# Neighbourhood attention: keys grouped by column strips, tokens reordered, nine second-stage units by seven products, an uneven share of filler

## The chip, the cores and the metric

One core of a Trainium2 chip runs the whole program. It has five engines that run their own instruction queues in order and meet by semaphores: TensorE (matmuls, written PE in the profile, its weight loads PEld), VectorE (DVE), ScalarE (ACT), GpSimd (POOL) and SyncE (SP), which here issues nearly all DMAs. Matmul results land in PSUM, in eight banks; everything else that the engines read or write lies in SBUF. The metric is the device time of one execution in microseconds; the time before is the median of three runs.

## The reference

One layer: an RMS norm, a projection of 1024 columns to q, k, v and a gate, a 2-D neighbourhood attention over a grid of 32 rows by 64 columns (2048 tokens, 16 heads of 64), a SiLU gate, an output projection with the residual, and a last RMS norm. A query sees 8 rows by 16 columns of keys, with a bias by relative position.

```python
h = rmsnorm(x, g)
proj = h @ w_in
q, k, v, gate = jnp.split(proj, 4, axis=-1)
# per query row r, keys of 8 rows from clip(r - 4), per 16 query columns 32 key columns
s = jnp.einsum('bnqhd,bknjhd->bhnqkj', qr, kr) * scale
s = jnp.where(col_valid, s + bias, NEG_INF)
p = jax.nn.softmax(s over all its keys)
o = jnp.einsum('bhnqkj,bknjhd->bnqhd', p, vr)
x = x + (o * jax.nn.silu(gate)) @ w_out
return rmsnorm(x, norm_f)
```

## The kernel before

All large products are done in three matmuls each (high by high, high by low, low by high part of float32 values rounded to float32r).

**Projection units.** A unit is 256 output columns of one kind: k, q and g (the gate) have four each, numbered j = 0 to 3, for two head pairs each; v has its own code. The 2048 tokens form four chunks c of 512. Stage one (`stage_one`) makes v and all twelve units for chunks 0 and 1, stage two (`stage_two`) makes v and the units of `units_two` for chunks 2 and 3. Both go through `seven_products`: a Strassen-Winograd scheme that gets a unit's 2 x 2 blocks (two column halves by two chunks) from seven block products of 4 x 3 matmuls of 128x512, with sums formed ahead on VectorE (`sum_`, `form`) and behind (`keep`, `add`, `out_`, `evac`). `give` splits or gates a result and stores it to DRAM with a lag. In stage one the results are multiplied by the reciprocal norm `rb[c]` on the way.

**Direct units.** The (kind, j, chunk) in `halves` that stage two leaves out are projected directly by `projections` and `group`: 24 matmuls for each column half and chunk. They are not done at once: together with the output projection (`outputs`) they are the *filler* of the attention.

**Attention.** `order` lists (head pair p, row block T); T counts 8 grid rows, whose keys lie in 11, 15, 15 or 12 rows (`KEY_ROWS`). First T = 0 for all eight pairs, then T = 1 and 2, then T = 3. Each entry gives two steps, of two column blocks C of 16 query columns each; so there are 64 steps and two more in which the last work runs out. A block C of 128 queries sees 24 or 32 key columns (`KEY_COLS`). Step i of the main loop does, in program order:

- `begin(i)`: loads for later steps are put on the SP queue (`load_k`, `load_e`, `load_v`, `load_sg`, each with a lag counted in filler matmuls), and `bias` adds mask and position table on GpSimd, L970;
- `feed`: filler matmuls, `amount[i]` of them in three portions, with `middle(i)` (query split `split_q`, next query load) between; the last portion goes on into an overdraft of up to 12 matmuls until 8 have passed since the last evacuation was issued (`calm`);
- `normalise(i - 1)`: the reciprocals of the softmax sums on VectorE (L1004) and the scaling on GpSimd (L1006);
- `turns(i - 2)`: transposes of the probabilities into PSUM (L1011), copied to SBUF by VectorE (L1036) and ScalarE (L1035);
- `scores(i)`: twelve matmuls (L988), then bias and negated maximum by one VectorE operation each (L995) and exponentials with sums on ScalarE (L998);
- `values(i - 2)`: the products with v (L1056), and in each odd step the gate multiplication (L1070) and the store of the result.

Transposes and products with v work on blocks of 4 key rows by 24 or 32 key columns, so the probabilities' contraction has 96 or 128 lines, and 72 or 96 where a block has only three rows; those are copied separately. For such blocks v must lie with rows and columns of one block in the partitions: `copy_v` copies v in DRAM from `vd` to `vc` once for each head pair, column block and half (64 DMAs in stages one and two), and `load_v` loads one tile for each column block. The tokens come in natural order for the projections; q and the gate are rearranged to blocks of 16 columns while they are evacuated (`tiled`, `blocked`), by runs of 16 values.

**Output.** `outputs` makes 16 tiles of 128 tokens: a tile's gated result is loaded and split (`split_og`, L1128 and L1129), 48 matmuls follow (L1250 to L1254) in two halves, `add_rows` adds the residual (L1161), and `finish` stores three later pieces of work with lags of 12, 24 and 44 filler matmuls: the reciprocal root of the last norm (`root`, eight small VectorE operations), the scaling (`scale`) and the two stores (`send`).

The order of the filler against the attention is a hand-written credit count:

```python
early = 96 * (12 - len(units_two)) + 192
amount = [early / 48] * 48 + [(384 - 30) / 18] * 18
```

With three units in `units_two` that is 1056 / 48 = 22 matmuls in each of the first 48 steps and 19.7 in the last 18.

## Time and profile before

| | |
|---|---|
| median of three runs | 1084.95 us (1084.85 to 1085.42) |
| the profiled execution | 1086.36 us, of it span 1084.5 us |
| granted TensorE clock | 0.999 |
| busy: TensorE, VectorE, ScalarE, GpSimd | 1071.1, 703.2, 531.2, 357.9 us |
| v of stage one, its products | 0 to 96 us, 96 to 327 us |
| v of stage two, its products | 327 to 414 us, 414 to 471 us |
| attention with filler | 471 to 1027 us |
| last output tiles | 1027 to 1084 us |

A profile row names a line of the kernel, an engine, an operation and the tiles written and read, with the count, the busy time, the mean length of one, and the idle time of the engine just before them with what ended it. A row of the table by stage has, for a stretch of the span, the busy time of each engine and the number of instructions in it, then the granted clock, the busy share of the DMA engines and the GB/s they moved. In the timeline a row begins with the start and the length; what stands in brackets is the idle time of the engine before it and what it had waited for.

### The profile page before, as it was taken

The numbers are of one execution on the slowest core, as the hardware profiler recorded it, in microseconds if no ns is written. First come the engines' busy times: TensorE is split into PE (matmuls) and PEld (weight loads), VectorE is DVE, ScalarE is ACT, GpSimd is POOL, SyncE is SP. The second block draws the span as 40 slices with busy tenths as digits, with TensorE's granted clock in tenths as the row PEclk, the third lists the DMA queues.
The fourth block names the chain that finished last, engine by engine and source line by source line (L and its number), as shares of the span: only waits on it lengthen the run. The fifth ranks groups of instructions, "written<-read, shape, count | busy, mean of one in ns | idle before, by whom it ended". The sixth has DMA issues, their size and how long they took to land.

```text
span 1084.5 us, 21929 instructions
## 1 busy us (share of the span) xinstructions
PE 1071.1 (99%) x7657; PEld 877.1 (81%) x7657; DVE 703.2 (65%) x1644; ACT 531.2 (49%) x1345; POOL 357.9 (33%) x474
## 2 busy tenths in 40 slices
PE   9999999999999999999999999999999999999997
PEld 6888888888888888887888888888888787888885
DVE  5376778778997535576555555664676786776643
ACT  7545334333434334346555555564576565665431
POOL 0000222312221000017545534444447656566200
PEclk9999999999999999999999999999999999999999
DMA  9633557574764366889868876886899787887442
GB/s 313 212 97 106 202 173 210 163 232 146 256 188 143 108 172 170 258 277 310 245 205 267 253 216 204 255 269 200 246 319 294 230 268 231 274 262 226 126 149 78
DMA packets 145901, 231.90 MB, mean 214 GB/s; under 512 B 13824, under 2 KB 61184, under 8 KB 145792
## 3 DMA queue, kind: packets, MB, share of 16 engines
q1 hardware_dynamic: 145648, 230.25, 68.2%
q8 instruction: 61, 1.00, 0.4%
q14 instruction: 48, 0.39, 0.1%
q10 hardware_dynamic: 144, 0.26, 0.1%
HBM read 171.73 MB, written 73.40 MB: 226 GB/s over the span
## 4 chain that ended last, share of the span: by engine, by line
PE 92%; DVE 3%; DMA 1%; ACT 1%; issue 1%; SPq 0%; POOL 0%; ACTq 0%; DVEq 0%; POOLq 0%
PE pp L411 23%; PE pv L531 16%; PE o L1056 8%; PE s L988 6%; PE pp L359 6%; PE pp L357 6%; PE pp L355 6%; PE po L1254 6%; PE po L1252 5%; PE po L1250 5%; PE ph L1011 5%; PE zp L1269 1%; DMA k_hi<-hi 1%; DMA land<-in_xt_dram 0%; DVE f L394 0%
## 5 line engine op out<-in xcount | busy, mean ns | idle before, releaser
L1006 POOL TENSOR_SCALAR x<-x,st 128x360 f32<-128x360 f32 (+5 forms) x256 | 143.0, 578 | 235.0 <-DVE st L1004 192.3
L970 POOL TENSOR_TENSOR em<-e,mk 128x480 f32<-128x480 f32 (+5 forms) x160 | 136.3, 886 | 138.3 <-DMA raw<-in_xt_dram 135.0
L998 ACT ACTIVATE x<-x,st 128x360 f32<-128x360 f32 (+5 forms) x256 | 151.8, 595 | 44.4 <-DVE st L995 44.4
L411 PE MATMUL pp<-h,f 128*128 128x512 f32 x480 | 155.4, 389 | 0.0
L430 POOL TENSOR_TENSOR tmp<-tmp,rb 128x512 f32<-128x512 f32 x36 | 58.9, 1637 | 270.6 <-DVE tmp L428 223.7
L411 PE MATMUL pp<-t,f 128*128 128x512 f32 x540 | 130.0, 390 | 0.3 <-DVE u L422 0.2
L995 DVE CUSTOM_DVE_ANT_0 x<-s,em 128x360 f32<-128x360 f32 (+5 forms) x256 | 124.0, 539 | 5.3 <-PE s L988 1.4
L411 PEld LDWEIGHTS pp<-t,f 128*128 128x128 f32 x540 | 101.2, 188 | 22.2 <-DVE u L422 1.2
L359 PE MATMUL pp<-h,w 128*128 128x512 f32 x288 | 115.1, 400 | 0.0
L357 PE MATMUL pp<-l,w 128*128 128x512 f32 x288 | 113.2, 393 | 0.0
L355 PE MATMUL pp<-h,w 128*128 128x512 f32 x288 | 113.1, 393 | 0.0
L1035 ACT ACTIVATE pta<-ph 96x256 f32<-96x256 f32 (+1 forms) x224 | 58.5, 333 | 104.3 <-PE ph L1011 104.3
L1036 DVE COPY pta<-ph 128x384 f32<-128x384 f32 (+3 forms) x128 | 60.7, 514 | 72.7 <-PE ph L1011 72.5
L411 PEld LDWEIGHTS pp<-h,f 128*128 128x128 f32 x480 | 90.1, 188 | 18.8
L1254 PE MATMUL po<-wol,gh 128*128 128x512 f32 x252 | 100.3, 398 | 0.0
L1252 PE MATMUL po<-woh,gl 128*128 128x512 f32 x252 | 98.9, 393 | 0.0
L1250 PE MATMUL po<-woh,gh 128*128 128x512 f32 x252 | 98.9, 392 | 0.0
L1056 PEld LDWEIGHTS o<-pta,vt 96*64 96x64 f32 (+2 forms) x1792 | 83.6, 137 | 17.2 <-issue 10.2
L1056 PE MATMUL o<-pta,vt 96*64 96x128 f32 (+4 forms) x1792 | 92.3, 254 | 1.4 <-DVE pta L1036 1.0
L411 PE MATMUL pp<-l,f 128*128 128x512 f32 x240 | 93.4, 389 | 0.0
L531 PE MATMUL pv<-wh,h 128*128 128x512 f32 x256 | 88.1, 390 | 0.0
L531 PE MATMUL pv<-wh,l 128*128 128x512 f32 x256 | 88.0, 389 | 0.0
(148 smaller groups left out, 1916.6 us busy)
## 6 DMA issues: line engine op xcount, KB each, us to landing
raw<-in_wg_dram SPq DMA_DIRECT2D x126, 256.0 KB, 5.1
e<-in_rpb_dram SPq DMA_DIRECT2D x54, 240.0 KB, 3.9
vt<-vc SPq DMA_DIRECT2D x64, 192.0 KB, 3.7
row<-in_xr_dram SPq DMA_DIRECT2D x32, 256.0 KB, 4.3
vd<-v SPq DMA_DIRECT2D x32, 256.0 KB, 3.0
k_hi<-hi SPq DMA_DIRECT2D x32, 256.0 KB, 2.6
k_lo<-lo SPq DMA_DIRECT2D x32, 256.0 KB, 3.8
vc<-vd SPq DMA_DIRECT2D x32, 256.0 KB, 4.4
```

Source lines behind the costliest of these rows:

```text
L355: nc.tensor.matmul(p, wh[w, b][:, cols], hh[k, c], start=(k == 0), stop=False)
L357: nc.tensor.matmul(p, wh[w, b][:, cols], hl[k, c], start=False, stop=False)
L359: nc.tensor.matmul(p, wl[w, b][:, cols], hh[k, c], start=False, stop=(k == NK - 1))
L411: nc.tensor.matmul(B[n, P], t[:, int(m == 2), c], x[k][int(m == 1)], start=P in (1, 6, 5) and k == 0 and m == 0, stop=k == 3 and m == 2, s ...
L531: nc.tensor.matmul(ps[t], a[:, o], b, start=k == 0 and m == 0, stop=k == NK - 1 and m == 2)
L970: (nc.gpsimd if attending[0] or not s else nc.vector).tensor_tensor(sh(t), E[p, s][:, u0 + 4:u1 + 4, v0 + 8:v1 + 8], sh(MK[0][:, m0:m0 + n ...
L998: nc.scalar.activation(X[i, C][s], X[i, C][s], AF.Exp, bias=st[:, s:s + 1], scale=-1.0, accum_out=st[:, 2 + s:3 + s])
L1006: nc.gpsimd.tensor_scalar(X[i, C][s], X[i, C][s], st[:, 4 + s:5 + s], 0.5, op0=OP.mult, op1=OP.mult)
L1056: nc.tensor.matmul(o[s * 64:s * 64 + 64, C * 128 + q0:C * 128 + q0 + nq], vt[C][:k, g - g0_, s * 64:s * 64 + 64], t[:k, at:at + nq], start ...
L1250: nc.tensor.matmul(p, gh, woh[q, j], start=(i == 0), stop=False)
L1252: nc.tensor.matmul(p, gl, woh[q, j], start=False, stop=False)
L1254: nc.tensor.matmul(p, gh, wol[q, j], start=False, stop=(i == NK - 1))
```

## The change

Seven things are changed together.

1. **Strips.** Keys are grouped by strips of 8 key columns over all key rows of the row block (11, 15 or 12), so a contraction has 88, 120 or 96 lines. `blocks(T)` becomes `strips(C)`; a column block has three or four strips, of which two concern all 128 queries and the others one half. Scores read k, and `bias` its table, by strips; `turns` copies each half in one operation; the queries of a block are ordered by two halves of 8 columns.
2. **Token order.** The host hands x over with the 64 columns of a grid row in the order (column within a strip, strip). v stored in this order already has, for each key row and column within a strip, its eight strips side by side, so `load_v` takes one tile of 8 strips for a head pair and row block, straight from `vd`; `copy_v`, `vc` and their 64 DMAs are gone, and the pool `vp` has two tiles of 1024 in place of four of 512.
3. **Evacuations.** k, q and the gate are put into their final order when PSUM is read (`of`, `lay`), now with a stride of 8 values; `rb` of chunks 0 and 1 is kept in k's order first and in the order of q and gate after `reorder_rstd`. Stage one therefore makes the four k units first. The gate multiplication of the attention needs no rearranging.
4. **Nine units in stage two.** `units_two` has j = 0 to 2, and `halves` only j = 3.
5. **Uneven filler.** 8.5 matmuls in each of the first 28 steps (and 8 more in each of the first three), the rest of the 480 evenly over the next 20, the last 18 as before.
6. **Overdraft.** 4.25 in place of 12.
7. **Roots.** While the attention runs, `root` is not queued with a lag but waits in a list for the next odd step (or the last steps), where `run_roots` runs it after 45% of the step's filler; scaling and stores follow 9 and 27 matmuls later.

```diff
-def blocks(T):
...
+def strips(C):
     out = []
+    for s in range(KEY_COLS[C][0] // 8, KEY_COLS[C][1] // 8):
+        halves = [h for h in range(2) if abs(2 * C + h - s) <= 1]
+        out.append((s, s - KEY_COLS[C][0] // 8, halves[0] * 64, len(halves) * 64))
     return out
...
+def reorder_rstd(c):
+    t = rbp([128, 512], F32, "rb")
+    nc.scalar.activation(t.rearrange("p (s r c) -> p s r c", r=8, c=8),
+                         rb[c].rearrange("p (r s c) -> p s r c", s=8, c=8), AF.Copy)
+    rb[c] = t
...
-    units_two = [(k, j) for j in range(1) for k in "kqg"]
-    halves = [(k, j, 1, c) for j in range(1, 4) for g in (("k", "q", "g") if j < 3 else ("k", "qg")) for c in (2, 3) for k in g]
+    units_two = [(k, j) for j in range(3) for k in "kqg"]
+    halves = [(k, j, 1, c) for j in range(3, 4) for g in ("k", "qg") for c in (2, 3) for k in g]
...
+    def of(kind, t):
+        return t.rearrange("p (r c s) -> p r s c", c=8, s=8) if kind == "k" else t.rearrange("p (n s) -> p s n", s=8)
+
+    def lay(kind, t):
+        return t.rearrange("p (r s c) -> p r s c", s=8, c=8) if kind == "k" else t.rearrange("p (s n) -> p s n", s=8)
...
-            nc.vector.tensor_tensor(U[n, i], B[n, P], U[n, 1], OP.add)
+            nc.vector.tensor_tensor(lay(kind, U[n, i]), of(kind, B[n, P]), lay(kind, U[n, 1]), OP.add)
...
-        us = [(k, j) for j in range(4) for k in "kqg"]
+        us = [("k", j) for j in range(4)] + [(k, j) for j in range(4) for k in "qg"]
...
-            if m and i in (1, 3, 5):
-                copies(0, 1)
+            if (m, i) == (4, 0):
+                reorder_rstd(0)
+                reorder_rstd(1)
...
+    def load_v(p, T):
         r0, r1 = KEY_ROWS[T]
+        must(*[("v", p // 4, t) for t in range(r0 // 2, (r1 + 1) // 2)])
+        rows = vd[p // 4][p % 4].rearrange("(k s) d -> k s d", s=8)[8 * r0:8 * r1]
+        VT[p, T] = t = vp([128, 1024], F32, "vt").rearrange("p (s d) -> p s d", s=8)
+        nc.sync.dma_start(t[:8 * (r1 - r0)], rows)
...
-                    nc.tensor.matmul(pst[s], qq[a, qs], kk[a, :r1 - r0, c0:c1], start=(m == 0), stop=(m == 2))
+                    nc.tensor.matmul(pst[s], qq[a, qs], kk[a, :r1 - r0, c0:c1].rearrange("p r (s c) -> p s r c", c=8), start=(m == 0), stop=(m == 2))
...
             for h in range(2):
-                four = sum(b[2] == 4 for b in halves_[h])
-                k = 4 * width(C)
+                n = len(halves_[h])
                 put = (lambda o, i_: nc.scalar.activation(o, i_, AF.Copy)) if h else nc.vector.tensor_copy
-                put(slots[:k, h, :2 * four], ph[h][:k, :128 * four].rearrange("p (n q) -> p n q", q=64))
-                if four < len(halves_[h]):
-                    k = halves_[h][four][2] * width(C)
-                    put(slots[:k, h, 2 * four:2 * four + 2],
-                        ph[h][:k, 128 * four:128 * four + 128].rearrange("p (n q) -> p n q", q=64))
+                put(slots[:k, h, :2 * n], ph[h][:k, :128 * n].rearrange("p (n q) -> p n q", q=64))
...
-        store(("y", n), 12, root)
-        store(("y", n), 24, scale)
-        store(("y", n), 44, send)
+        if ended[0]:
+            store(("y", n), 12, root)
+            store(("y", n), 24, scale)
+            store(("y", n), 44, send)
+        else:
+            roots.append((clock[0] + 8, n, root, scale, send))
+
+    roots = []
+    ended = [False]
+
+    def run_roots():
+        while roots and (roots[0][0] <= clock[0] or ended[0]):
+            _, n, root, scale, send = roots.pop(0)
+            root()
+            store(("y", n), 9, scale)
+            store(("y", n), 27, send)
...
-    amount = [early / 48] * 48 + [(384 - 30) / 18] * 18
+    first = 8
+    amount = [8.5] * 28 + [(early - 3 * first - 8.5 * 28) / 20] * 20 + [(384 - 30) / 18] * 18
+    calm_debt = amount[0] / 2
+    for i in range(3):
+        amount[i] += first
...
-        while credit[0] > 0 or credit[0] > -12 and clock[0] - state["event"] < calm:
+        while credit[0] > 0 or credit[0] > -calm_debt and clock[0] - state["event"] < calm:
...
-        if 0 < i <= N:
-            p, T, cs = pairs[i - 1]
-            later_loads(load_v(p, T, cs[0]) + load_v(p, T, cs[1]), 0, 2)
+        if i % 2 == 0 and i < N:
+            load_v(*order[m])
...
         quiet[0] = i % 2 == 1 or i >= N
+        if quiet[0]:
+            run_roots()
```

More of the change, by code (lines that the diff above doesn't have):

```diff
@@ L93, in build, with vh @@
     qp = pool("qp", 4)
-    vp = pool("vp", 4)
+    vp = pool("vp", 2)
+    vhalf = []
+    def vh(shape, dt, nm):
+        if not vhalf:
+            t = vp([128, 1024], dt, nm)
+            vhalf.extend((t[:, :512], t[:, 512:]))
+        return vhalf.pop(0)
     sp = pool("sp", 2)
@@ L627, in also @@
                     split_v(0, 1, 1)
-                    L2["x12"] = [vp([128, 512], F32, "land") for _ in range(4)]
+                    L2["x12"] = [vh([128, 512], F32, "land") for _ in range(4)]
                     for k in range(4):
@@ L792, in pair @@
                     do[b]()
-                if u and ts != (12,) and b % 2:
-                    copies(1, 1)
         def both(*fs):
@@ L1006, in normalise, with split @@
                 nc.gpsimd.tensor_scalar(X[i, C][s], X[i, C][s], st[:, 4 + s:5 + s], 0.5, op0=OP.mult, op1=OP.mult)
-    def turn(dst, i, C, s, blk, q0, nq):
-        g, lr, nr = blk[:3]
-        w = width(C)
-        nc.tensor.transpose(dst[:nr * w], X[i, C][s][q0:q0 + nq, lr * w:(lr + nr) * w],
-                            ident[q0:q0 + nq, q0:q0 + nq])
-    def split(T):
-        bl = blocks(T)
-        return [b for b in bl if b[4] == 128], [b for b in bl if b[4] == 64]
+    def split(C):
+        return [b for b in strips(C) if b[3] == 128], [b for b in strips(C) if b[3] == 64]
     def turns(i):
         p, T, cs = pairs[i]
-        full, part = split(T)
-        halves_ = [full + [b for b in part if b[3] == 64 * h] for h in range(2)]
+        k = 8 * (KEY_ROWS[T][1] - KEY_ROWS[T][0])
         for C in cs:
+            full, part = split(C)
+            halves_ = [full + [b for b in part if b[2] == 64 * h] for h in range(2)]
             t = PT[i, C] = pa([128, 768], F32, "pta")
@@ L1047, in values @@
         o = O[p, T]
-        g0_ = KEY_ROWS[T][0] // 4
-        vt = {C: VT.pop((p, T, C)) for C in cs}
+        vt = VT[p, T]
         for C in cs:
@@ L1356, in build @@
             values(i - 2)
+    ended[0] = True
+    store(("roots",), 8, run_roots)
     while next(outs, 0) != 0:
@@ L1377 @@
         "x": np.ascontiguousarray(xp),
[L1378 to L1379 removed]
+        "xr": np.ascontiguousarray(xc),
+        "xt": np.ascontiguousarray(xc.T),
         "wg": np.ascontiguousarray(wg),
```

122 lines of the change are left out of this document (45 added, 77 removed).

## The prediction

> **What bounds the kernel now.** I read the busy time of each engine first, then the same by stage, then the chain of waits, then single steps of the attention in order of time.
>
> ```profile
> PE 1071.1 (99%) x7657; PEld 877.1 (81%) x7657; DVE 703.2 (65%) x1644; ACT 531.2 (49%) x1345; POOL 357.9 (33%) x474
> ```
> ```profile
> core 0: us, PE busy (x) PEld busy (x) DVE busy (x) ACT busy (x) POOL busy (x), PEclk, DMA share, GB/s
> ...
> 96.00:315.00 219.00, 218.65 (x964) 180.39 (x963) 181.49 (x269) 84.02 (x163) 54.04 (x33) 1.00 0.61 190
> ...
> 416.00:471.00 55.00, 55.00 (x245) 45.53 (x244) 32.16 (x49) 16.66 (x29) 3.44 (x4) 1.00 0.81 249
> ...
> 490.00:623.00 133.00, 131.77 (x1244) 108.00 (x1243) 71.85 (x242) 75.79 (x239) 73.98 (x119) 1.00 0.82 257
> 623.00:803.00 180.00, 179.91 (x1869) 147.65 (x1869) 105.67 (x300) 101.90 (x297) 81.87 (x114) 1.00 0.77 241
> ```
> TensorE sets the end in every stage: 218.65 of 219 us in stage one's products, 55 of 55 in stage two's, 179.91 of 180 in the middle of the attention. Every other engine has room there, most of all in the attention, where VectorE is busy 105.67 of 180 us. So a matmul less is a matmul's time less, as long as the others keep up with a TensorE that comes round sooner.
>
> The price of one 128x512 matmul, from a stretch of the chain in stage two, and from two filler matmuls of the attention with seven issue intervals between them:
> ```profile
> 414.20 54.41 PE pp L411 x240
> ```
> ```profile
> 647.33 0.39 PE L355 MATMUL pp<-h,w 128*128 128x512 f32 x1
> ...
> 648.92 0.39 PE L357 MATMUL pp<-l,w 128*128 128x512 f32 x1
> ```
> 54.41 / 240 = 0.227 us, and 1.59 / 7 = 0.227 us: the same in both stages (the 0.39 us are one matmul's length, the matmuls overlap).
>
> **The change, part by part.**
>
> *Six more units by seven products.* A unit done directly takes 4 groups of 24 matmuls, 96; by seven products 7 x 12 = 84. Units go from three to nine, so 6 x 12 = 72 matmuls vanish: 72 x 0.227 = **16.3 us less**. It is certain by count. It is also a move: the attention loses 576 matmuls of filler (130.7 us) and stage two gains 504 (114.3 us). Stage two's units now take 55 us for three with VectorE at 32.16, so six more fit there under TensorE; I cost that at nothing.
>
> *The attention's steps get short.* A step (two query blocks of one head pair and row block) is filler, transposes, scores, products with v. Its own work on TensorE is read between the last filler matmul before it and the first after it, in a step with 11 key rows and in one with 15:
> ```profile
> 540.17 0.39 PE L357 MATMUL pp<-l,w 128*128 128x512 f32 x1
> ...
> 543.50 0.50 PE L359 MATMUL pp<-h,w 128*128 128x512 f32 x1
> ```
> ```profile
> 640.99 0.39 PE L357 MATMUL pp<-l,w 128*128 128x512 f32 x1
> ...
> 644.93 0.50 PE L359 MATMUL pp<-h,w 128*128 128x512 f32 x1
> ```
> ```profile
> L1056 PE MATMUL o<-pta,vt 96*64 96x128 f32 (+4 forms) x1792 | 92.3, 254 | 1.4 <-DVE pta L1036 1.0
> ...
> L1011 PE MATMUL ph<-ident,x 64*96 64x64 f32 (+2 forms) x1408 | 58.4, 223 | 0.0
> ```
> 3.33 - 0.23 = 3.10 us and 3.94 - 0.23 = 3.71 us. Strips keep both counts (1792 and 1408: seven strips to a step pair in place of six or eight blocks, 56 a head pair either way) and only even them out, so I move a quarter microsecond from the long steps to the short: 3.35 and 3.46 us. Filler was 1056 / 48 = 22 matmuls a step. Now it is 16.5 in steps 0 to 2, 8.5 to step 27, 10.9 to step 47 (480 in all); the last 18 keep 19.7. So a step without any stall takes 8.5 x 0.227 + 3.35 = **5.28 us** (row block 0, to step 15), **5.39 us** (steps 16 to 27), 10.9 x 0.227 + 3.46 = **5.93 us** (28 to 47), where 8 to 9 us were.
>
> *What VectorE must do in such a step.*
> ```profile
> L995 DVE CUSTOM_DVE_ANT_0 x<-s,em 128x480 f32<-128x480 f32 x64 | 39.5, 654 | 2.5 <-PE s L988 0.4 <-POOL x L1006 0.2
> ...
> L995 DVE CUSTOM_DVE_ANT_0 x<-s,em 128x360 f32<-128x360 f32 x64 | 31.4, 528 | 0.5 <-PE s L988 0.2
> ```
> ```profile
> L1036 DVE COPY pta<-ph 128x384 f32<-128x384 f32 (+3 forms) x128 | 60.7, 514 | 72.7 <-PE ph L1011 72.5
> ...
> L496 DVE SCALAR_TENSOR_TENSOR ql<-qr,qh 128x512 fp32r<-128x512 f32 x32 | 22.1, 691 | 27.1 <-ACT qh L495 27.1
> L1070 DVE TENSOR_TENSOR og<-o,sgt 128x512 f32<-128x512 f32 x32 | 22.0, 687 | 4.2 <-PE pp L359 2.6 <-PE o L1056 1.1
> ...
> L1004 DVE RECIPROCAL st<-st 128x2 f32<-128x2 f32 x128 | 14.6, 151 | 3.0 <-ACT x L998 3.0
> ```
> By busy time over count, for 15 key rows: 2 x 0.617 + 2 x 0.491 for the score reductions, 2 x 0.474 for the copies of the transposes, 2 x 0.114 reciprocals, half of 0.69 (og) and half of 0.69 (ql): 4.08 us. The filler's own VectorE work comes on top:
> ```profile
> L1161 DVE TENSOR_TENSOR y<-po,xr 128x512 f32<-128x512 f32 x30 | 20.7, 689 | 35.2 <-PE po L1254 35.1
> L1129 DVE TENSOR_TENSOR gl<-ograw,gh 128x512 fp32r<-128x512 f32 (+1 forms) x32 | 21.3, 708 | 9.9 <-ACT gh L1128 9.9
> L175 DVE TENSOR_TENSOR w<-raw,w 128x512 fp32r<-128x512 f32 x36 | 26.8, 748 | 21.3 <-ACT w L174 21.3
> L1191 DVE SCALAR_TENSOR_TENSOR y<-y,st,acc 128x512 f32<-128x512 f32 x15 | 14.7, 979 | 0.3
> ```
> ```profile
> 904.82 0.22 DVE L1180 SCALAR_TENSOR_TENSOR st<-st 128x1 f32<-128x1 f32 x1
> ...
> 905.72 0.16 DVE L1184 SCALAR_TENSOR_TENSOR st<-st 128x1 f32<-128x1 f32 x1
> ```
> Up to step 27: eight evacuations of k and gate, seven weight splits, four splits of x (two operations each) and some eight of the sixteen w_out splits, 31 operations of about 0.73 over 31 steps: 0.73 us a step. From step 28: four output tiles, each 2 x 0.69 + 2 x 0.71 + 0.98 and the eight small operations of the root (the last five take 1.06, so I put 1.7), 5.5 us, and eight more splits: 28 us over 20 steps, 1.4 us. So VectorE needs 4.81 of 5.39 us (**89%**), then 5.5 of 5.93 (**93%**). In row block 0 it spent 71.85 us in 15.5 steps, 4.6 a step with the old filler, below 87% of 5.28. There GpSimd is as close: 73.98 / 15.5 = 4.8 of 5.28 us, but its results are used a step later. ScalarE gains: the one-block copies (96 of the 224 at L1035) go.
>
> *What a full VectorE costs TensorE.* The nearest rows are pairs of steps in which it was fullest, and one step in which it was late:
> ```profile
> 799.50:817.20 17.70, 17.61 (x183) 14.37 (x182) 14.82 (x39) 12.48 (x35) 9.76 (x13) 1.00 1.01 309
> 853.30:872.80 19.50, 19.05 (x189) 15.27 (x189) 15.50 (x50) 11.29 (x33) 13.98 (x17) 1.00 0.87 272
> 872.80:890.90 18.10, 17.76 (x210) 14.59 (x210) 14.32 (x41) 11.83 (x37) 10.08 (x16) 1.00 0.90 273
> ```
> ```profile
> 913.76 0.68 DVE L1161 TENSOR_TENSOR y<-po,xr 128x512 f32<-128x512 f32 x1
> ...
> 914.49 0.29 PEld L988 LDWEIGHTS s<-kt,qh 64*128 64x128 f32 x3 [0.42 <-DVE y L1161]
> 914.50 0.99 DVE L1036 COPY pta<-ph 128x384 f32<-128x384 f32 x2
> ...
> 915.52 0.30 PEld L988 LDWEIGHTS s<-kt,qh 64*128 64x128 f32 x4 [0.55 <-ACT pta L1035]
> ```
> At 84% TensorE lost 0.09 us in two steps, at 79% 0.45 and 0.34: 0.05 to 0.23 a step. The second fence shows how: one late output addition ahead of the copies, and the scores, which take the PSUM banks that the copies free, waited twice. At 89 to 93% no row exists. Bounds: no stall; or VectorE held to the 84% shown, which makes the steps 5.48, 5.73 and 6.55 us, 13 x 0.20 + 12 x 0.34 + 20 x 0.62 = 19 us. I take 0.3 a step, a little over the largest row, since operations of 0.7 us fall unevenly into a spare of 0.4 to 0.6: 32 x 0.3 + 13 x 0.1 = **10.9 us**.
>
> *Edits at about nothing.* The second arrangement of v (64 copies) and two of three loads a step go; they were queue work and DMA, not TensorE's. Loads in the short steps: at 15 key rows a head pair moves 2.4 MB a pair of steps and the filler some 0.7, about 290 GB/s against 309 shown without a stall; what is late first would be the k tiles, asked for two steps ahead. The shifted roots and the smaller overdraft of filler (4.25 for 12) change when, not how much; within plus or minus 2 us. Order and layout: scores read k in runs of 8, the score bias reads its table in runs of 8, and evacuations read PSUM with a stride of 8.
> ```profile
> L970 POOL TENSOR_TENSOR em<-e,mk 128x360 f32<-128x360 f32 x44 | 40.2, 935 | 0.0
> ...
> L970 POOL TENSOR_TENSOR em<-e,mk 128x352 f32<-128x352 f32 x15 | 13.9, 949 | 1.3 <-DVE st L995 1.3
> ```
> ```profile
> L313 DVE TENSOR_TENSOR tmp<-pp,rb 128x512 f32<-128x512 f32 x8 | 5.5, 688 | 3.7 <-PE pp L411 3.7
> ...
> L315 DVE TENSOR_TENSOR tmp<-pp,rb 128x512 f32<-128x512 f32 x4 | 2.8, 688 | 1.2 <-PE pp L411 1.2
> ```
> Runs of 24 (360 columns) cost GpSimd no more an element than runs of 32 (352), and reading PSUM in runs of 16 (L315) costs VectorE what a plain read costs (L313). By these rows all of it is free, and I take that; the other bound is a doubled read, the third rival.
>
> **The sum.** Span 1084.5 - 16.3 + 10.9 = 1079.1; with the 1.86 us around it (1086.36 in all) 1081.0. That execution lay 1.4 above the median of 1084.95, so **1079.5** for the median.
>
> **Rivals.** (1) *No stall:* the spare of 0.4 to 0.6 us absorbs everything, as nearly so at 799.5. 1084.95 - 16.3 = 1068.7. Against it: the waits at 914 and 915. (2) *VectorE is the bound in the attention and the kernel is slower:* its in-order queue cannot be used beyond the 84% shown, the copies of the transposes come late every step and the scores wait for banks; the 19 us above give 1084.95 - 16.3 + 19 = 1088, and up to 1095 if ScalarE's exponentials are late with it. It decides from 16.3 / 45 = 0.36 us a step. (3) *The strided PSUM reads are slow.* Stage one has VectorE at 181.49 of 219 us; six such reads a unit in twelve units, each 0.688 longer, are 49.5 us, 231 in all: 12 us over TensorE, 1079.5 + 12 = 1091. For it speaks only that a stride for each single element is not in the trace. [...] (4) *The matmuls are not saved:* excluded by the count of 84 against 96, which the page's 1260 and 864 instances (15 and 9 units) bear out.
>
> **How the numbers follow.** Forecast (a stall of 0.2 to 0.36 us a step, 1074 to 1083) 0.42; rival 1 (below 1074) 0.12; rival 2 0.36; rival 3 0.08; the rest beyond. 0.2% is 2.2 us, about what a measurement here can tell. Faster: 0.12 and 0.40 of the forecast, 0.52; within 0.2%: 0.07, out of the seam to rival 2; slower 0.41. The range 1067 to 1095 takes in no stall and the far end of rivals 2 and 3; the forecast's own is 1074 to 1083.
>
> **What would show it.** Right: 1764 matmuls by seven products and 288 direct; stage two longer by 114 us; steps of 5.4 to 6.2 us up to step 47 with TensorE busy over 94% there, and VectorE at 85 to 90%. Rival 2: TensorE below 93% in that stretch, waits of scores and of v products for the copies, summing to over 16 us. Rival 3: L422 and L428 well above 690 ns and TensorE idle in stage one. What would make me wrong without either: k tiles late, seen as waits of scores for a DMA.

## The result and the profile after

The changed kernel takes **1097.17 us** (1096.46 to 1100.15, four runs) against 1085.09 of the kernel before on the same chip (1084.85 to 1085.42, four runs): a ratio of 1.0113, 95% interval 1.0100 to 1.0127. It is slower by 12 us. The prediction said 1079.5, with a range of 1067 to 1095.

The engines of the changed kernel, then busy times by stretch (the columns are those of the same view in the prediction):
```profile
PE 1073.2 (98%) x7585; PEld 871.4 (80%) x7585; DVE 743.1 (68%) x1716; ACT 535.8 (49%) x1269; POOL 353.5 (32%) x474
```
```profile
core 0: us, PE busy (x) PEld busy (x) DVE busy (x) ACT busy (x) POOL busy (x), PEclk, DMA share, GB/s
414.00:585.50 171.50, 171.50 (x758) 142.08 (x757) 103.74 (x165) 55.46 (x99) 2.87 (x4) 1.00 0.46 146
602.00:605.00 3.00, 1.50 (x20) 1.18 (x22) 2.03 (x11) 2.09 (x8) 2.44 (x5) 0.75 0.95 294
605.00:610.00 5.00, 4.57 (x38) 3.68 (x36) 3.81 (x14) 3.59 (x13) 5.00 (x8) 0.50 1.00 270
610.00:613.00 3.00, 3.00 (x19) 2.16 (x15) 0.83 (x3) 1.09 (x3) 2.13 (x5) 0.50 1.05 395
613.00:616.00 3.00, 3.00 (x39) 2.17 (x40) 1.96 (x7) 1.13 (x3) 2.71 (x6) 0.88 0.85 320
605.00:1038.00 433.00, 423.72 (x4717) 338.90 (x4713) 307.02 (x976) 272.60 (x768) 281.97 (x418) 0.99 0.78 242
```
The 72 matmuls are gone (7585 instructions on TensorE for 7657). Stage two's products run from 414 to 585.5 us with TensorE full. The attention is where it was lost: TensorE is busy 97.9% of the stretch from 605, though VectorE works only 71% of it, and from 605 to 613 the clock granted to TensorE is 0.50: the 28 products with v of one step take 2.61 us from 608.25, where the next step's 28 take 1.44 from 615.78. A busy TensorE is therefore no sign that nothing was lost, since matmuls at half clock count as busy (3.00 of 3.00 us from 610 to 613).

What came ahead of that slow clock, in order of time (start, length, engine, line; in brackets the idle time before and what ended it):
```profile
600.42 0.68 DVE L350 TENSOR_TENSOR lo<-pp,hi 128x512 fp32r<-128x512 f32 x1
...
601.02 1.28 DVE L179 TENSOR_TENSOR w<-raw,w 128x512 fp32r<-128x512 f32 x2
...
602.23 0.22 DVE L994 RECIPROCAL st<-st 128x2 f32<-128x2 f32 x2
...
602.57 2.01 POOL L996 TENSOR_SCALAR x<-x,st 128x264 f32<-128x264 f32 x4 [18.83 <-DVE st L994]
...
603.10 0.12 PEld L1015 LDWEIGHTS ph<-ident,x 64*88 64x88 f32 x2 [2.26 <-POOL x L996]
```
The weight loads of the first transposes wait 2.26 us for GpSimd's normalisation (the array itself stands idle for 1.84), that waits for VectorE's reciprocals, and those stand in VectorE's queue behind the filler's k part and weight splits. Filler that would have covered it was cut from 22 matmuls a step (and an overdraft of 12) to 16.5 (and 4.25).

Then the score matmuls themselves. The costliest group and the next, before and after (busy us, mean ns):
```profile
L988 PE MATMUL s<-kt,qh 64*128 64x480 f32 x128 | 22.9, 414 | 0.4 <-ACT pta L1035 0.4
L988 PE MATMUL s<-kt,qh 64*128 64x360 f32 x128 | 18.0, 346 | 0.0
```
```profile
L978 PE MATMUL s<-kt,qh 64*128 64x480 f32 x128 | 28.9, 439 | 1.3 <-DVE pta L1019 1.3
L978 PE MATMUL s<-kt,qh 64*128 64x360 f32 x128 | 24.1, 382 | 1.9 <-DVE pta L1019 1.1 <-ACT pta L1018 0.7
```
Work of the same count and shape takes longer. Whether that is the new way of reading k or a wait inside the record can't be told from these rows.

One table serves all that follows. A step's own time on TensorE is read from the start of the last filler matmul before it to the start of the first after it; unlike in the prediction the one filler interval of 0.23 us in it is not taken off. These are sums in us over 64 steps, in four groups, with step i the one that turns scores i - 2. The last group holds six filler matmuls of the last step, the same in every row. The last columns give the shorter steps that recur in a group, read as steps that wait for nothing:
```
                 2-17   18-29  30-49  50-65   all     a step undisturbed
                 T=0    T=1,2  T=1,2  T=3             (T=0, T=1/2, T=3)
before           55.9   46.7   79.5   57.0   239.1    3.32  3.86  3.40
after            69.0   50.2   85.1   57.6   261.8    3.50  3.87  3.58
b_strip_scores   56.3   48.2   80.9   57.7   243.2    3.39  3.98  3.51
a_start          58.0   56.6   85.5   57.6   257.6    3.48  3.88  3.58
a_out            57.3   55.0   84.9   56.4   253.6    3.41  3.74  3.48
n_base           57.6   51.9   84.9   56.4   250.9    3.41  3.74  3.48
n_noq            55.9   49.0   79.8   55.8   240.5    3.41  3.74  3.48
n_noem           57.5   49.6   80.0   56.4   243.6    3.41  3.74  3.48
six_best         55.6   45.1   76.9   56.1   233.6    3.41  3.74  3.48
```
Before to after the steps' own time grew by 22.7 us. With 16.3 saved that makes 6.4 of the 10.2 us by which the span grew (1084.5 to 1094.7). The other 3.8 are by difference. About 2 of them are ten filler matmuls under the slow clock (0.50 from 610 to 613 and from 658.8 to 661.5), which start 0.40 to 0.60 us apart from 610.8 and from 658.8 (0.23 usual), and 1.3 are one output matmul that waits for a low part from VectorE at 888 us.

### The profile page after: what moved, and what is told of

Its sections match the earlier page's. It is cut to its first block, busy times and chain, and to the rows that moved or that the text cites. A ratio compares the mean times of both kernels' runs of the same rounds, so it can differ in the third digit from the quotient of the medians.

```text
span 1094.7 us, 21517 instructions
## 1 busy us (share of the span) xinstructions
PE 1073.2 (98%) x7585; PEld 871.4 (80%) x7585; DVE 743.1 (68%) x1716; ACT 535.8 (49%) x1269; POOL 353.5 (32%) x474
## 5 line engine op out<-in xcount | busy, mean ns | idle before, releaser
L419 PE MATMUL pp<-h,f 128*128 128x512 f32 x672 | 217.5, 389 | 0.0
L419 PE MATMUL pp<-t,f 128*128 128x512 f32 x756 | 181.8, 389 | 0.3 <-DVE u L432 0.2
L419 PEld LDWEIGHTS pp<-t,f 128*128 128x128 f32 x756 | 141.8, 188 | 30.5 <-DVE u L432 1.2
L1033 PEld LDWEIGHTS o<-pta,vt 120*64 120x64 f32 (+2 forms) x1792 | 84.9, 139 | 19.0 <-issue 15.9
L978 PE MATMUL s<-kt,qh 64*128 64x480 f32 (+5 forms) x512 | 92.4, 387 | 7.5 <-DVE pta L1019 4.0
L402 DVE TENSOR_TENSOR f<-raw,f 128x512 fp32r<-128x512 f32 x105 | 80.1, 763 | 25.0 <-ACT f L401 25.0
L1033 PE MATMUL o<-pta,vt 120*64 120x128 f32 (+5 forms) x1792 | 93.8, 257 | 0.5 <-ACT pta L1018 0.3
L1019 DVE COPY pta<-ph 120x384 f32<-120x384 f32 (+5 forms) x128 | 62.5, 514 | 42.6 <-PE ph L1015 42.2
L540 PE MATMUL pv<-wl,h 128*128 128x512 f32 x256 | 87.9, 389 | 0.0
L1018 ACT ACTIVATE pta<-ph 120x384 f32<-120x384 f32 (+5 forms) x128 | 52.1, 458 | 67.6 <-PE ph L1015 67.6
```

The costliest lines, as they stand in the source:

```text
L402: nc.vector.tensor_tensor(t[:, 1], src, t[:, 0].bitcast(F32), OP.subtract)
L419: nc.tensor.matmul(B[n, P], t[:, int(m == 2), c], x[k][int(m == 1)], start=P in (1, 6, 5) and k == 0 and m == 0, stop=k == 3 and m == 2, s ...
L540: nc.tensor.matmul(ps[t], a[:, o], b, start=k == 0 and m == 0, stop=k == NK - 1 and m == 2)
L978: nc.tensor.matmul(pst[s], qq[a, qs], kk[a, :r1 - r0, c0:c1].rearrange("p r (s c) -> p s r c", c=8), start=(m == 0), stop=(m == 2))
L1033: nc.tensor.matmul(o[s * 64:s * 64 + 64, C * 128 + q0:C * 128 + q0 + nq], vt[:k, strip, s * 64:s * 64 + 64], t[:k, at:at + nq], start=firs ...
```

## The experiments

Theories: **A**, reading k in runs of 8 makes the score matmuls slower. **B**, VectorE's sum of work sets the short steps (the forecast's stall). **C**, the start of the attention is uncovered. **D**, loads whose delay is counted in filler matmuls come late when a step has 8.5 of them. **E**, VectorE has room, but stands in order behind ScalarE. Every ratio is to the kernel before on the same chip; the interval is 95%. That kernel's own medians ran from 1085.1 to 1086.6 us over the chips used, so a difference in us between runs of different chips is good to about one.

**The reading of k, and the start.** Edits: in the kernel before
```diff
-nc.tensor.matmul(pst[s], qq[a, qs], kk[a, :r1 - r0, c0:c1], ...
+nc.tensor.matmul(pst[s], qq[a, qs], kk[a, :r1 - r0, c0:c1].rearrange("p r (s c) -> p s r c", c=8), ...
```
as b_strip_scores, the reverse in the changed kernel as a_plain_scores, and `first = 8` to `first = 20` as a_start.

> The kernel before, with one edit: the score matmuls read k's columns in strips of 8 (runs of 8 elements) in place of whole rows of 24 or 32. The scores then stand in strip order while bias and masks stay in row order, and everything else is untouched. Theory A (the strip order makes the score matmuls themselves slower, by some 0.1 us in a step with 11 key rows and 0.2 in one with 15): 48 x 0.15 + 16 x 0.1 = 6 to 9 us more, 1091 to 1094, with the records of a 128x480 score matmul at 439 ns and of a 128x360 at 382 (414 and 346 before). Theory B (the score matmuls only look longer in the changed kernel because they wait for VectorE's banks): no change, 1085, records as before.

1090.08 us, 1.0041 (1.0029 to 1.0053): 4.3 us more.
```profile
L988 PE MATMUL s<-kt,qh 64*128 64x480 f32 x128 | 23.6, 429 | 0.2 <-ACT pta L1035 0.2
L988 PE MATMUL s<-kt,qh 64*128 64x360 f32 x128 | 19.7, 370 | 0.0
```
In a kernel in which hardly anything waits, 414 became 429 ns and 346 became 370, and the steps' own time rose by 4.1 us, nearly all of the loss. A holds, but at 4.3 us, under its 6 to 9; theory B's "no change" falls. The changed kernel's records (439 and 382) hold its waits and its slow clock as well.

> The changed kernel, with one edit undone: the score matmuls read k by whole rows again (the scores' columns are then in row order where the rest expects strips). Theory A: the same 6 to 9 us come back, 1088 to 1091. Theory B (VectorE and ScalarE set the step there, so that TensorE only waits longer): 1096 to 1098.

1089.99 us (1088.14 to 1095.37), 1.0044 (1.0028 to 1.0060): 7 us less than the changed kernel, as A has it, but its runs spread by 7 us. Something else in it comes and goes.

> The changed kernel, with 20 extra filler matmuls in each of the first three steps in place of 8, the 36 taken from the 20 steps before the last 18 (10.9 filler matmuls a step become 9.1). Theory C (the 2.3 us wait at the start of the attention and the half clock after it cost 5 to 9 us): that wait is covered by 2.7 us more filler, the clock stays at 1.00, 1088 to 1092. Rival (the time lost there would be lost anyhow, since the later steps have too little filler): 1096 to 1099, with steps 28 to 47 longer by what the first ones give back.

1088.93 us, 1.0034 (1.0022 to 1.0046): 8.2 us less. C holds. The first group falls from 69.0 to 58.0 us. Of these 11.0 us the first transposes' step gives 6.3 (9.92 to 3.67). Another 3.3 are step 10 (6.77 to 3.51), where the changed kernel's scores waited for a k tile at 654 us, which they do not here; that this edit mended that too is not shown. And 50.2 rises to 56.6: in this profile a stall later on took part of it back.
```profile
711.43 0.32 SPq L942 DMA_DIRECT2D sgt<-sgd  x1
```
```profile
720.38 0.69 DVE L1049 TENSOR_TENSOR og<-o,sgt 128x512 f32<-128x512 f32 x1 [3.70 <-DMA sgt<-sgd]
...
721.13 0.18 PEld L978 LDWEIGHTS s<-kt,qh 64*128 64x128 f32 x1 [1.32 <-DVE og L1049]
...
722.18 0.50 PEld L978 LDWEIGHTS s<-kt,qh 64*128 64x128 f32 x3 [0.87 <-DVE pta L1019]
...
727.24 0.63 PE L365 MATMUL pp<-l,w 128*128 128x512 f32 x1
```
The gate tile was asked for at 711.43, behind the two k tiles, after a delay of 15 filler matmuls (9 and 13 for the k tiles). VectorE waited for it until 720.38, the copies and the scores behind it, and then the filler ran under a slow clock (0.53 granted from 726 to 729; 0.63 us a matmul where 0.39 is usual). That is D's case.

**How much of it is the count of units.** a_six: `units_two` over `range(2)`, `halves` from j = 2, `amount` 14.5 and 17 for 8.5 and 10.9, and with it the overdraft, half of the first, 7.25 for 4.25.

> The changed kernel with six units of stage two by seven products in place of nine: 36 matmuls more in all (8.2 us), 288 of filler more in the attention (14.5 a step in place of 8.5, 17 in place of 10.9). If the losses come from what does not depend on the length of a step (A alone, or the start): 1097 + 8 = 1105 at most, 1098 to 1105. If they come from short steps in which VectorE and ScalarE are late (B): those losses of 11 to 20 us go, 1085 to 1094.

1085.45 us (1084.54 to 1089.67), 1.0007 (0.9998 to 1.0015). 36 matmuls more and yet 11.7 us less than nine units: the losses hang on the filler in a step, at the start (step 2 takes 5.51 us for 9.92) and later. Its steps 18 to 29 have no wait at all (46.6 us, 3.88 each) at about 7 us a step.

**Three mends, singly and together**, all on a_start:
```diff
 a_out
-nc.tensor.matmul(pst[s], qq[a, qs],
+nc.tensor.matmul(pst[s].rearrange("p (s r c) -> p r s c", r=r1 - r0, c=8), qq[a, qs],
                  kk[a, :r1 - r0, c0:c1].rearrange(...)    # by rows again
 a_loads
-later_loads(load_e(nx[0]), 5, 3); later_loads([kh, kl], 9, 4); later_loads([load_sg], 15, 0)
+later_loads(load_e(nx[0]), 2, 1); later_loads([kh, kl], 4, 2); later_loads([load_sg], 1, 0)
 a_norm
-middle(i) ... normalise(i - 1); turns(i - 2)
+turns(i - 2); normalise(i - 1); middle(i)
```

> The kernel with 20 extra filler matmuls in each of the first three steps (1088.9), and the score matmuls read k by whole rows again while they write PSUM in strips of 8, so that the scores stand in the order that the rest expects. Theory A (reading the moving operand in runs of 8 is what costs; writing PSUM in runs of 8 is free): 4 to 7 us less, 1082 to 1085, a 128x480 score matmul back from 442 to about 415 ns. Rival (the strips cost on whichever side they stand): 1088 to 1090, records as they were; if writing costs more than reading, 1092 and over.

1089.17 us (1083.78 to 1095.03, twelve runs), 1.0033 (1.0014 to 1.0052): no gain over a_start that can be told in the time, though the matmul is mended:
```profile
L978 PE MATMUL s<-kt,qh 64*128 64x480 f32 x128 | 26.4, 411 | 1.5 <-DVE pta L1020 0.6 <-DVE og L1050 0.6 <-DVE y L1141 0.4
```
At 64x480, writing PSUM in runs of 8 costs nothing (411 ns for 414 plain), reading k in such runs does (429 in b_strip_scores). The undisturbed steps fell to 3.41, 3.74 and 3.48 us. By that, 64 steps should save some 7 us (16 x 0.07 + 32 x 0.14 + 16 x 0.10); the profiled run's saved 4.0 (257.6 to 253.6). Steps 24, 25 and 29, which wait for VectorE, are as long as before within 0.2 us. The twelve runs differ by 11 us, so the median can't tell such a gain.

> The kernel with 20 extra filler matmuls in each of the first three steps (1088.9), and the loads of a step asked for earlier: the gate tile after 1 filler matmul in place of 15, the k tiles after 4 and 6 in place of 9 and 13, the bias table after 2 and 3 in place of 5 and 8. Theory D (these delays are counted in filler matmuls, and with 8.5 a step in place of 22 a delay of 15 lasts into the next step, so that the gate tile lands after it is wanted): the 3.7 us wait at 720 us and the slow clock after it go, 5 to 7 us less, 1082 to 1084. Rival (the DMA queues are full there, and asking earlier only moves the wait to another tile): 1088 to 1090.

1088.03 us, 1.0019 (1.0011 to 1.0028): 0.9 us less, which is no clear gain, where 5 to 7 were expected. The wait at 720 is gone (step 22 from 7.92 to 3.88 us), but in the profile step 29 now takes 7.10 for 5.85. Taken by itself D was a miss; with a_out's edit beside it, in n_base below, it was worth 5.8, and a_out's beside it 4.6.

> The kernel with 20 extra filler matmuls in each of the first three steps (1088.9), and in each step the reciprocals with the normalisation, and the split of q, are put behind the copies of the transposes in the queues of VectorE and ScalarE, where they stood ahead of them. Theory E (the copies wait in order behind operations that wait for ScalarE's exponentials of the step before; a step cannot be shorter than scores, reductions, exponentials, split of q, copies, which is 5.7 to 6.3 us with 15 key rows): the steps 18 to 47 lose their waits, 32 x 0.2 to 0.3 = 6 to 9 us less, 1080 to 1083. Theory B (VectorE's sum of work sets the step): no change, 1088 to 1090. A third way: the normalised scores are now late for the next step's transposes, 1092 and over.

1095.54 us, 1.0089 (1.0076 to 1.0102): 6.6 us longer than a_start, the third way. TensorE's waits from 690 to 905 us, in a_start and in a_norm (waiter, waited for, us, times, longest):
```profile
PEld ph L1015 <- POOL x L996: 4.6, 13, 0.8
```
```profile
PEld ph L1015 <- POOL x L996: 13.1, 30, 1.3
```
With the normalisation moved back, the next step's transposes wait for GpSimd, 8.5 us more in this stretch; the waits for VectorE's copies of the transposes fall by 3.1 only (9.0 to 5.9). The wait has another name and is larger.

> The three edits of the other runs of this call together, on the kernel with 20 extra filler matmuls in each of the first three steps. If A, D and E each hold and add up: 1088.9 - 5.5 - 6 - 7 = 1070, which is what 72 matmuls less alone would give (1085 - 16.3 = 1069). If B holds: 1080 or over.

1089.25 us, 1.0030 (1.0019 to 1.0041). Not 1070: a_norm's loss eats the gain of the other two.

**Without a_norm, and E put to the test.** n_base is a_start with a_out's and a_loads' edits. n_dve has in addition
```diff
-nc.scalar.activation(h, t, AF.Copy)              # q, weights, x, k, attention output
+nc.vector.tensor_scalar(h, t, 1.0, None, op0=OP.mult)
```
during the attention, and n_dve_norm a_norm's order too.

> The nine-unit kernel with three mends and nothing else: 20 extra filler matmuls in the first three steps, PSUM written in strips by the score matmuls, the step's loads asked for earlier. If the mends add up where they do not overlap: 1083 to 1086. If the waits of steps 18 to 47 take over what they give (a step there cannot get shorter whatever is taken out of TensorE): 1086 to 1089.

1083.38 us, 0.9975 (0.9965 to 0.9985): faster than the kernel before. With the three mends it is 13.8 us less than the changed kernel.

> The kernel of n_base, and during the attention the high part of every split (q, weights, x, k, attention output) is copied by VectorE in place of ScalarE, so that VectorE's low part no longer waits for ScalarE, which comes to it only after the exponentials of the step before. VectorE gets some 60 operations of 0.4 to 0.7 us more up to step 47. Theory E (the waits come from VectorE standing in order behind ScalarE): shorter than n_base by 3 to 8 us although VectorE does more. Theory B (VectorE's work sets the step): longer than n_base, by 4 to 15 us.

1098.28 us, 1.0113 (1.0099 to 1.0127): 14.9 us longer than n_base. E's forecast of a shorter time fails, but the run can't part order from sum: the edit also gives VectorE 93 operations and 52 us more (796.6 for 744.5). Single steps lost their wait (step 25 from 5.06 to 3.76 us), others got longer ones (step 27 from 5.00 to 7.13).

> The kernel of n_dve, with the reciprocals, the normalisation and the split of q behind the copies of the transposes, so that no copy waits for an exponential any more. Theory E: shorter again than n_dve, 1075 to 1080. Theory B: no gain over n_dve. Third way (GpSimd's normalisation now comes late for the next transposes, behind its bias additions of 5.9 us): within 2 us of n_dve or longer.

1104.15 us, 1.0187 (1.0168 to 1.0206): longer again, by 5.9 us.

**Sum or order.** In n_extra_late and n_extra_early the following stands in each of the first 48 steps at its end, or ahead of `normalise`:
```diff
+for _ in range(3):
+    nc.vector.tensor_tensor(ones, ones, ones, OP.mult)
```

> The kernel of n_base (1083.4), with three small multiplications of a 128x128 tile on VectorE (some 0.7 us together, result not used) at the end of each of the first 48 steps, behind the score reductions and the output gating, where no TensorE operation of the step waits for them. If VectorE's sum of work sets the steps: as much longer as n_extra_early, 15 to 30 us. If what counts is only what stands ahead of the copies of the transposes: 0 to 5 us longer.

> The kernel of n_base, with the same three multiplications on VectorE in the first 48 steps, but just ahead of the reciprocals and the copies of the transposes, for which the scores wait. If the order counts: the copies are 0.7 us later wherever VectorE comes to them late already, 10 to 25 us longer and far more than n_extra_late. If the sum counts: the same as n_extra_late. If VectorE has room in most steps: under 5 us for both.

1109.66 us, 1.0217 (1.0201 to 1.0233), and 1132.51 us, 1.0435 (1.0417 to 1.0453). The dose was larger than meant, 76.8 and 72.5 us of VectorE in 144 operations, 1.5 to 1.6 us a step:
```profile
L1357 DVE TENSOR_TENSOR ones<-ones 128x128 f32<-128x128 f32 x144 | 76.8, 534 | 3.3
```
```profile
L1346 DVE TENSOR_TENSOR ones<-ones 128x128 f32<-128x128 f32 x144 | 72.5, 503 | 3.3
```
Less the 1083.4 of n_base, 26 us against 49: the same work costs about twice as much ahead of the copies as behind the reductions. The stretch 700 to 860 us in n_base, n_extra_late and n_extra_early:
```profile
700.00:860.00 160.00, 153.38 (x1828) 120.96 (x1828) 127.85 (x383) 111.82 (x305) 115.51 (x158) 1.00 0.81 261
```
```profile
700.00:860.00 160.00, 144.84 (x1712) 114.46 (x1709) 148.21 (x426) 104.64 (x287) 99.98 (x139) 0.98 0.75 240
```
```profile
700.00:860.00 160.00, 136.44 (x1555) 107.11 (x1554) 131.62 (x383) 96.97 (x265) 87.28 (x125) 0.96 0.70 225
```
VectorE (the third busy time) reaches 148.21 of 160, 93%, when the work stands where no TensorE operation of the step waits for it, and 82% when it stands ahead of the copies, with far more lost. So there is no ceiling at 84%; the sum counts, and the place counts as much.

**What stands ahead of the copies.** n_noq leaves out the split of q (all scores use the first head pair's q), n_noem GpSimd's bias additions after the first head pair of each row type.

> The kernel of n_base, with the split of q left out after the first (all scores use the first head pair's q): per two steps 0.61 us of ScalarE and 0.69 us of VectorE less, which stand ahead of the copies in the odd steps. If these odd steps wait because of it: 1.0 us back in some 14 of them, 6 to 12 us shorter, with the waits of the even steps left. If the waits come from the filler's splits and evacuations: under 3 us.

1072.38 us, 0.9876 (0.9862 to 0.9891): 11.0 us less than n_base. The split's own work on VectorE and ScalarE is gone with it, not only its place in the queue.

> The kernel of n_base, with GpSimd's bias additions (six operations, 5.5 to 5.9 us in a row for each head pair and row type) left out after the first head pair of each type (later ones use that pair's bias). If these bursts make the waits (VectorE's additions from two SBUF tiles took 1.2 to 1.5 us in place of 0.69 beside them, and the normalisation stands behind them): 4 to 10 us shorter. If not: under 2 us.

1075.54 us, 0.9906 (0.9891 to 0.9920): 7.8 us less, without one VectorE operation taken away: the same 1716 operations keep VectorE busy for 735.3 us in place of 744.5. The transposes' weight loads also wait less for GpSimd's normalisation (2.5 us for 8.1), which stands behind the additions in GpSimd's queue; how the 7.8 divides between the two was not told apart. In n_base, step 24, VectorE's low parts run beside GpSimd's additions:
```profile
727.80 6.41 POOL L960 TENSOR_TENSOR em<-e,mk 128x360 f32<-128x360 f32 x6
...
729.47 1.14 ACT L1108 ACTIVATE gh<-ograw 128x512 fp32r<-128x512 f32 x2
...
730.00 0.80 PE L1016 MATMUL ph<-ident,x 64*120 64x64 f32 x20
...
730.12 2.54 DVE L1109 TENSOR_TENSOR gl<-ograw,gh 128x512 fp32r<-128x512 f32 x2 [1.13 <-ACT gh L1108]
...
732.71 0.86 DVE L1020 COPY pta<-ph 120x256 f32<-120x256 f32 x2
...
733.16 1.44 PE L1034 MATMUL o<-pta,vt 120*64 120x128 f32 x28 [1.02 <-DVE pta L1020]
```
The transposes were done by 730.9; the copies that the v products need began at 732.71. Ahead of them stood two low parts of a filler tile, which first waited 1.13 us for ScalarE (busy with the exponentials) and then took 1.27 us each beside GpSimd's six additions, where the prediction's row has 0.71.

**Versions that compute the reference.** n_best is n_base with q split where it is evacuated and stored as two tensors, and the third column type's bias additions behind the normalisation; six_out is a_six with n_base's mends, six_best six_out with n_best's edits.

> Six units by seven products in place of nine, with the same three mends as n_base (20 extra filler matmuls in the first three steps, PSUM written in strips, loads earlier). Six units without them took 1085.5 with few waits. If a step with 14.5 filler matmuls keeps its waits covered, what the score matmuls give back is time: 1085.5 - 4 to 6 = 1079 to 1082, faster than the kernel before by 0.4 to 0.6%. If not: 1085.

1077.26 us, 0.9920 (0.9906 to 0.9933), 8.2 us less than a_six, more than expected. The three mends come through where the steps are covered; how they share the 8.2 was not told apart.

> The kernel of n_base (1083.4), with q split into its two parts where it is evacuated and stored as two tensors (32 loads and 32 stores of 256 KB more, no split in the steps), and the third column type's bias additions put behind the normalisation, so that GpSimd's burst ahead of it has four operations in place of six. If the cause of the waits is what stands ahead of the copies: near n_noq's 1072.4 and a little under it, 1069 to 1075. If the second q tensor's loads are late or VectorE's moved work stalls the stages: 1076 to 1083.

1076.65 us (1074.36 to 1079.02), 0.9903 (0.9886 to 0.9919): 6.7 us off n_base, not the 11 to 18 of the two runs that leave work out; the moved split must still be done, and the loads of q doubled.

> The same two edits on six_out (1077.3), whose steps had few waits left: 1073 to 1077. If nine units are mended in full they come out under this by up to 36 x 0.227 = 8 us; if their steps still wait, within 2 us of it.

**1074.30 us** (1073.41 to 1076.56), 0.9891 (0.9876 to 0.9906), the lowest median here of a kernel that computes the reference. Its row for 700 to 860 us:
```profile
700.00:860.00 160.00, 158.56 (x1734) 129.64 (x1730) 114.25 (x350) 101.42 (x275) 103.12 (x143) 1.00 0.88 278
```
Nine units do 36 matmuls less and are no faster: the medians differ by 2.4 us, and the runs overlap. In n_best's profile the steps still wait, with TensorE busy 154.91 of the same 160 us.

## Why the prediction was wrong

**Right.** 72 matmuls fewer, at the same price. Stage two's six units more cost nothing beyond their matmuls (171.50 of 171.50 busy). The strided PSUM reads are free, and rival 3 is out: the doubled read that it was priced by was the author's bound, and no run shows it. Stage one's products show TensorE full, and the additions that read PSUM with a stride take 689 ns where the plain ones of the kernel before (L422) take 688.
```profile
96.00:327.00 231.00, 230.56 (x1015) 189.98 (x1014) 191.04 (x282) 90.81 (x174) 56.85 (x35) 1.00 0.52 161
```
```profile
L432 DVE TENSOR_TENSOR u<-pp,p 128x512 f32<-128x512 f32 x42 | 29.0, 689 | 24.6 <-PE pp L419 24.6
```
The shift from long steps to short ones was right in sign and smaller: with k read by rows (n_base against before, steps that wait for nothing), the 11-row steps rose by 0.06 to 0.09 us and the 15-row steps fell by 0.12 to 0.19, for a quarter.

**Wrong, first: "Edits at about nothing", "scores read k in runs of 8".** The step took GpSimd's and VectorE's rows (360 against 352 columns, L315 against L313) for a matmul's reading. They price other engines, and runs of 24 and 16. On TensorE the records of the two largest groups grow by 15 and 24 ns a matmul, and the kernel by 4.3 us in all (b_strip_scores). The other bound, a doubled read, was kept for PSUM alone; for k it should have stood in the range.

**Wrong, second: "The shifted roots and the smaller overdraft of filler (4.25 for 12) change when, not how much; within plus or minus 2 us."** At the start of the attention, when is how much: the first transposes hang on a chain from the scores over VectorE, ScalarE, VectorE and GpSimd, and filler is all that covers it. Twelve matmuls more in each of three steps gave 8.2 us (a_start), and 6.3 us in the step of that wait. The array was idle for 1.84 us of these; the rest fell into the stretch at half clock behind the wait (0.50 from 605 to 613), a cost that no term of the sum had.

**Wrong, third: the stall term, 10.9 us out of VectorE's 89 to 93%.** Its sum of VectorE's work was nearly right. In the changed kernel's steps 16 to 27 and 28 to 47:
```profile
689.40:761.40 72.00, 71.69 (x850) 56.55 (x850) 53.67 (x168) 51.69 (x140) 44.57 (x66) 1.00 0.87 269
761.40:896.80 135.40, 131.00 (x1463) 103.02 (x1462) 106.05 (x316) 89.80 (x247) 98.58 (x136) 1.00 0.82 257
```
53.67 / 12 = 4.47 and 106.05 / 20 = 5.30 us a step, where the sum had 4.81 and 5.5. What failed is what the term made of it: spare time in the step's length less this sum, with 84% as a ceiling. There is no such ceiling (93% in n_extra_late), and VectorE was at 75 and 78% here. Yet steps 2 to 49 of the changed kernel stand 25 us over steps that wait for nothing (204.3 - 16 x 3.50 - 30 x 3.87 - 2 x 3.62), the start and the slow clock included, where the term had 10.9. What remains in steps 18 to 49 of n_base is 136.8 - 119.2 = 17.6 us (30 steps of 3.74, two of 3.52). That the bound has nearly this for the steps 16 to 47 (12 x 0.34 + 20 x 0.62 = 16.5) is luck, since the ceiling that it stands on is not there. The mechanism is the queue: the copies stand behind the split of q (n_noq, 11.0 us, its work included) and behind low parts that are longer beside GpSimd's additions (1.27 us for 0.71; n_noem, 7.8 us, the normalisation's part included); the two overlap, and were not left out together. Rival 2 named these late copies and their 0.36 us a step, and gave 1088 to 1095 for them; it was the right mechanism, but for the ceiling, with the first two errors missing from its sum, and it had too small a chance (0.36) beside the forecast's milder stall. The sign that the prediction named for being right, TensorE busy over 94%, held in these two stretches (71.69 of 72 and 131.00 of 135.40) and so told nothing. Single removals do not add up to an account of the 12 us: a_start gave 8.2, a_plain_scores 7.2, and n_base 13.8 with the loads as well.

**"What would make me wrong without either: k tiles late, seen as waits of scores for a DMA."** This came true once in the changed kernel's profile, in step 10:
```profile
654.36 0.40 PE L978 MATMUL s<-kt,qh 64*128 64x264 f32 x2 [0.92 <-DMA kt<-k_lo]
...
655.96 1.06 PE L978 MATMUL s<-kt,qh 64*128 64x352 f32 x4 [1.05 <-DVE og L1049]
```
That step took 3.3 us more than in a_start, where no score waits for a DMA and the late tile is the gate's. Both tiles are asked for after delays counted in filler matmuls, which last longer when filler is thin. By itself the mend of the delays gave 0.9 us, beside a_out's 5.8. That the runs of a_out spread by 11 us and those of n_base by 1.6 fits a load that sometimes lands in time; it was not traced run by run, and a_start, with the same delays as a_out, spread by 3.9 in five runs.

## What to carry to other kernels

When work is taken from the engine that sets the end, what covered the others' latency goes with it: before counting the saving, list what the in-order queues hold ahead of each operation that this engine waits for, and how long the chain through them is against the new step. Delays that are written in units of the removed work (filler, loop turns) must be set anew. And where two causes make the same wait, mending one can show nothing: a mend of the operand order that showed no gain by itself in nine units was worth keeping, since it gave 4.6 us once the delays of the loads were mended.

## Hardware that I had not expected

A 64x480 score matmul that reads its moving operand in runs of 8 elements takes 429 ns against 414, and a 64x360 one 370 against 346 (b_strip_scores against before). Writing its PSUM result in runs of 8 instead costs nothing at 64x480 (411 in a_out). At 64x360 a_out has 321 for 322 with q's low part; with its high part it has 365 for 346, with 2.1 us of waits before that group, and n_noq, which writes alike and waits less there (0.4 us), has 350.

TensorE's clock went slow behind short waits. In the changed kernel it was 0.50 from 605 to 613, behind 1.84 us of idle array up to 603.10, and it fell again around 0.92 and 1.05 us of idle array within 2.6 us:
```profile
653.00:656.00 3.00, 1.03 (x15) 0.57 (x9) 0.79 (x4) 0.86 (x2) 1.24 (x2) 1.00 0.58 183
656.00:660.00 4.00, 3.98 (x37) 3.16 (x38) 2.41 (x11) 2.25 (x8) 2.01 (x4) 0.76 0.77 210
```
In a_start it was 0.50 from 722 to 726, behind 0.98 and 0.54 us of idle array that ended at 721.13 and 722.18. The length of a wait does not decide by itself: in the changed kernel the array was idle for 1.28 us up to 888.79 and for 1.27 us up to 908.19, and the granted clock stayed at 1.00 from 887 to 892 and from 904 to 912. What does decide is not shown here.

VectorE's low parts of a filler tile took 1.27 us each beside GpSimd's additions in n_base's step 24, where the row of the kernel before has a mean of 0.71. In the changed kernel the two that start at 760.96 and 761.97, beside five additions that run from 758.71 to 764.28, take 1.09 and 1.59 us; the two from 781.16, with nothing on GpSimd beside them, take 0.69 each. All thirty together have a mean of 765 ns in n_base, 710 in n_noem, and 709 in six_out, which keeps the additions. n_noem puts 7.8 us on GpSimd's additions as a whole, of which this is one part.
